# A mixture-of-experts block on one core: one-hot gate rows all on VectorE, gates in four tensors, gathers dealt out by a weighted count

## The chip, the cores and the metric

The kernel runs on one core of one Trainium2 chip. The metric is the device time of one execution in microseconds; lower is better. The core has five engines with a queue each: TensorE (PE, with its weight loads as PEld), VectorE (DVE), ScalarE (ACT), GpSimd (POOL) and SyncE (SP, which here only issues DMAs). An engine takes its instructions in order; engines meet through semaphores.

## The reference, cut to what matters

Two transformer blocks run on 512 tokens of width 1024. The first ends in a product-key expert layer, which is where the change lies:

```python
g = jax.nn.softmax(best_s, axis=-1)                 # 8 heads x 16 chosen experts per token
u = expert_u[idx]                                   # idx = i * 128 + j, out of 16384 experts
act = jax.nn.gelu(jnp.einsum('cd,chkd->chk', xb, u), approximate=False)
w = (g * act).astype(xb.dtype)
return jnp.einsum('chk,chkd->cd', w, expert_v[idx])
```

The kernel treats the tokens in two ways. For the first 128 tokens it gathers the chosen rows of `u` and `v`. For the other 384 (`TD`) it computes the layer densely over all 16384 experts: expert block `b` (0 to 127) holds 128 experts, and a gate that is zero for an expert that was not chosen multiplies the activation.

## The kernel before

**Gate build (about 456 to 644 us).** It makes the dense gates, a matrix of 128 i by 128 j for each of the 384 tokens. Tokens go in 48 groups of 8 (`GS`). `gate_hot(g)` builds three tiles: `oj` and `oi`, one-hot rows of the two indices in fp16 (line 996, VectorE, 128x1024 each), and `og`, `oi` times the gate value (line 1003, 128x1024 out, fp32). Line 1003 runs on GpSimd in every third group (`OGP = 3`) and on VectorE in the others. `oj` and `og` have two buffers (`OGB`), `oi` one. `gate_sum(g)` multiplies them on TensorE, two fp16 matmuls a token (lines 1019 and 1020), into a PSUM bank of four tokens, and ScalarE copies each bank into the staging tile `st` (line 1021): it reads the bank in its own order (token, then i) and writes each element 64 elements (256 bytes) from the one before. `st` holds 64 tokens (`ST`) and has two buffers; when it is full, SP stores its 4 MB in one DMA into the HBM tensor `gates` (line 1023). There are six such stores.

Between the groups TensorE also computes 22 of the `u_side(b)` blocks: 24 matmuls each (lines 199 to 201), whose weights SP loads in pieces of 256 KB (line 93), ScalarE rounds to a high part `wh` (line 111) and GpSimd, in this stretch, subtracts to a low part `wl` (line 112). `Stream` keeps four loads (`WR`) and five split pieces (`WH`) ahead.

**Expert loop (about 644 to 1606 us).** Iteration `b` computes `u_side(b + 34)` (24 matmuls, as long as `b + 34 < 128`, so for b up to 93) and `v_side(b)` (18 matmuls, `vac`). `gate_load(b)` brings 192 KB of gates, 128 rows by six pieces of 256 bytes; `weigh(b)` multiplies them with the activations (line 1052) and splits the product (lines 1054, 1055). Here VectorE makes the low parts of line 112.

In the same loop run the gathered tokens: 256 `units`, 128 rows of `u` and 128 of `v`, each 512 KB by an indirect DMA from GpSimd's queue (line 1077). At most seven row tiles exist (`ROWS`), and a row is worked off five gathers later (`LAG`) by one VectorE instruction over 128x1024 (line 1083 for `u`, 1091 for `v`). How many are issued by iteration b is `due`: an equal number per iteration, all of them by b = 119. At b = 120 (`B_END`) the first 128 tokens get their final norm. What remains of the loop, and the second block, stand behind it.

The lines that deal out the gathers and lay out the gates are:

```python
due = min(len(units), -(-(b + 1) * len(units) // B_END))
gd = nc.dram_tensor("gates", (TD // ST, P, P, ST), FT, kind="Internal").ap()
```

Of the kernel before, what the change touches and what calls it, by code (L numbers as in the profile page):

```python
# [9 lines left out]
FT = mybir.dt.float32  # L10
FR = mybir.dt.float32r
F16 = mybir.dt.float16
# [3 lines left out]
AF = mybir.ActivationFunctionType  # L16
# [4 lines left out]
P = 128  # L21
# [11 lines left out]
TD = S - P  # L33
AA = 36
AHEAD = 34
ST = 64
ROWS, LAG = 7, 5
GS = 8
# [12 lines left out]
LA = 4  # L51
ADA_U = 2
ADA_M = 2
OGP = 3
OGB = 2
U_PRE = 4
B_END = 120
# [100 lines left out]
def body(ctx, tc, a):  # L158
    nc = tc.nc
    V, A, G, T = nc.vector, nc.scalar, nc.gpsimd, nc.tensor  # L160

    def pool(st, name, bufs=1, side="left", **kw):
        return st.enter_context(tc.tile_pool(name=name, bufs=bufs, side=side, reuse_waits="tile", **kw))
# [18 lines left out]
    def rstd(ss, n, inv, nm, bias=None, half=None):  # L182

        u = small.tile([P, n], FT, name=f"rs_u{nm}", tag=f"rs_u{n}")
        last["sqrt"] = A.activation(u, ss, AF.Sqrt, scale=inv, bias=eps if bias is None else bias).ins
        t = small.tile([P, n], FT, name=f"rs_t{nm}", tag=f"rs_t{n}")
        V.tensor_scalar(t, ss, -0.5 * inv, -0.5 * EPS if half is None else half, op0=OP.mult, op1=OP.add)
        r = small.tile([P, n], FT, name=f"rs_r{nm}", tag=f"rs_r{n}")
        V.reciprocal(r, u)
        if n == 1:  # L190
            V.scalar_tensor_tensor(u, r, r, t, op0=OP.mult, op1=OP.mult)
        else:
            V.tensor_mul(u, r, r)
            V.tensor_mul(u, u, t)
        V.scalar_tensor_tensor(r, u, 1.5, r, op0=OP.add, op1=OP.mult)
        return r
# [161 lines left out]
    def rope(pl, ps, raw, rot, cos, sin, nm, rows=slice(0, P), tag="ps", eng=G):  # L358

        pr = ps.tile([P, S], FT, name=f"{nm}pr", tag=tag)  # L360
        T.matmul(pr, con[:, rot - C_RM:rot - C_RM + P], raw, start=True, stop=True)
        t = pl.tile([P, S], FT, name=f"{nm}rt", tag="rt", bufs=2)
        u = pl.tile([P, S], FT, name=f"{nm}ru", tag="ru", bufs=RB)
        eng.tensor_tensor(u[rows], raw[rows], cos[rows], op=OP.mult)
        V.tensor_mul(t[rows], pr[rows], sin[rows])
        V.tensor_add(t[rows], t[rows], u[rows])
        return t

    def rope_swap(pl, raw, cos, sin, nm, eng=G):

        t = pl.tile([P, S], FT, name=f"{nm}rt", tag="rt", bufs=2)
        u = pl.tile([P, S], FT, name=f"{nm}ru", tag="ru", bufs=RB)
        for p0 in range(0, P, 32):
            p1 = p0 + 32 if p0 % 64 == 0 else p0 - 32
            nc.scalar.dma_start(t[p0:p0 + 32], raw[p1:p1 + 32])
        eng.tensor_tensor(u, raw, cos, op=OP.mult)
        V.tensor_mul(t, t, sin)
        V.tensor_add(t, t, u)
        return t
# [86 lines left out]
    i = A.activation(crow, crow, AF.Silu)  # L466
# [34 lines left out]
    with ExitStack() as s1:  # L501
# [10 lines left out]
        for n in range(2):  # L512
            pt = ps.tile([P, 512], FT, name=f"cs{n}", tag="ps")
# [3 lines left out]
        for b0 in (0, 2):  # L517
# [7 lines left out]
            t = rstd(ss, 2, 1.0 / D, f"n1{b0}")  # L525
            r1 += [t[:, 0:1], t[:, 1:2]]
        for b in range(NB):
# [3 lines left out]
            else:  # L531
                i = V.tensor_scalar(xn, x[:, b], r1[b], None, op0=OP.mult)
            if b == 0:
                order.enter_context(tc.issue_after(i.ins))
            for k0 in range(0, KD, 4):
                pt = ps.tile([P, 4, P], FT, name=f"xpt{b}_{k0}", tag="ps")
# [5 lines left out]
        for k in range(KD):  # L542
# [8 lines left out]
            t = p0.tile([P, S], FT, name=f"h1{k}", tag="ht", bufs=2)  # L551
            V.tensor_scalar(t, xnT[:, k], mod[:, k + 8:k + 9], mod[:, k:k + 1], op0=OP.mult, op1=OP.add)
            i = A.activation(hT[:, k], t, AF.Copy)
# [38 lines left out]
        for i in (2, 3):  # L592
# [3 lines left out]
            if i == 2:  # L596
# [13 lines left out]
                for f in (2, 0, 1):  # L610
                    pt = ps.tile([P, S], FT, name=f"lpt{f}", tag="ps")
                    for b in range(NB):
                        T.transpose(pt[:, b * P:(b + 1) * P], lat[:, b, f * P:(f + 1) * P], ident)
                    g = vec[:, V_QN + f:V_QN + f + 1]
# [8 lines left out]
        t = rope_swap(pb, raw_ka, tabs[:, 0], tabs[:, 1], "ka")  # L623
        q_split(t, ks[:, 0], ks[:, 1])
        raws = {0: raw_copy(acc[6], "rawq0")}
        for i in range(4):
            if i < 3:
                raws[i + 1] = raw_copy(acc[7] if i == 0 else qa[i + 1], f"rawq{i + 1}")
            t = rope_swap(pb, raws[i], tabs[:, 0], tabs[:, 1], f"q{i}")
            q_split(t, qs[:, 0, i], qs[:, 1, i])  # L630
            if i == 0:
                t = rope(pb, ps, raw_kr, C_RM, tabm[:, 1], tabm[:, 2], "kr", rows=slice(64, P))
# [5 lines left out]
        for h in range(8):  # L638
            if h % 2 == 0:
                w = ws.get(("qup", h // 2))  # L640
            pt = ps.tile([P, S], FT, name=f"qu{h}", tag="ps")
# [5 lines left out]
        for h in range(8):  # L647
            if h % 4 == 0:
                w = ws.get(("kup", h // 4))
            pt = ps.tile([P, S], FT, name=f"kup{h}", tag="ps")  # L650
# [4 lines left out]
        for b in range(NB):  # L655
            pt = ps.tile([P, 512], FT, name=f"vup{b}", tag="ps")
# [303 lines left out]
    for q in (1, 0, 2):  # L960
        pt = ps.tile([P, 512], FT, name=f"ixT{q}", tag="ps")
# [15 lines left out]
    gp32 = gp.rearrange("p t c -> p (t c)").bitcast(FT)  # L977


    gd = nc.dram_tensor("gates", (TD // ST, P, P, ST), FT, kind="Internal").ap()  # L980
    ps = ps.then(pA=2, pG=4, rest=2)
    s1 = ExitStack()
    pg = pool(s1, "pgb", OGB)
# [7 lines left out]
    def gate_hot(g):  # L991

        tt = slice(g * GS, (g + 1) * GS)

        def hot(out, q):
            V.tensor_tensor(out, iT[:, q, tt].rearrange("p (s t) -> p s t", t=4)[:, :, None].to_broadcast([P, GS // 4, P, 4]),
                            ioth[:, None].to_broadcast([P, GS // 4, P, 4]), op=OP.is_equal)
        oj = pg.tile([P, GS // 4, P, 4], F16, name=f"oj{g}", tag="oj")
        hot(oj, 1)
        oi = pg.tile([P, GS // 4, P, 4], F16, name=f"oi{g}", tag="oi", bufs=1)  # L1000
        hot(oi, 0)
        og = pg.tile([P, GS, P], FT, name=f"og{g}", tag="og")
        (G if g % OGP == 0 else V).tensor_tensor(og.rearrange("p (s t) i -> p s t i", t=4),  # L1003
                        oi.rearrange("p s i t -> p s t i"),
                        gp32[:, tt].rearrange("p (s t) -> p s t", t=4)[:, :, :, None].to_broadcast([P, GS // 4, 4, P]),
                        op=OP.mult)
        return g, oj, og

    stage = {}

    def gate_sum(g, oj, og):
        n, t0 = divmod(g * GS, ST)
        if t0 == 0:
            stage[n] = pg.tile([P, P, ST], FT, name=f"st{n}", tag="st", bufs=2)
        for h in range(GS // 4):
            pt = ps.tile([P, 4, P], FT, name=f"pG{g}_{h}", tag="pG")
            for t in range(4):
                o = og[:, 4 * h + t].bitcast(F16).rearrange("p (i w) -> p i w", w=2)
                T.matmul(pt[:, t], oj[:, h, :, t], o[:, :, 1], start=True, stop=False)  # L1019
                T.matmul(pt[:, t], oj[:, h, :, t], o[:, :, 0], start=False, stop=True)  # L1020
            A.activation(stage[n][:, :, t0 + 4 * h:t0 + 4 * h + 4].rearrange("p i t -> p t i"), pt, AF.Copy)  # L1021
        if t0 + GS == ST:
            nc.sync.dma_start(gd[n], stage.pop(n))

    hot = []
    NG = TD // GS
# [6 lines left out]
    while hot:  # L1033
        gate_sum(*hot.pop(0))
# [3 lines left out]
    pg = pool(s1, "pg", 2)  # L1038
# [5 lines left out]
    gates = {}  # L1044

    def gate_load(b):
        gates[b] = pg.tile([P, TD], FT, name=f"gt{b}", tag="gt", bufs=4)
        nc.sync.dma_start(gates[b].rearrange("p (n t) -> p n t", t=ST), gd[:, :, b].rearrange("n j t -> j n t"))

    def weigh(b):  # L1050
        w = pg.tile([P, TD], FT, name=f"w{b}", tag="w", bufs=1)
        V.tensor_mul(w, acts[:, b % AA], gates.pop(b))  # L1052
        wh, wl = (pg.tile([P, TD], FR, name=f"ww{c}{b}", tag=f"ww{c}", bufs=KL + 1) for c in "hl")
        A.activation(wh, w, AF.Copy)  # L1054
        last["w"] = V.tensor_tensor(wl, w, wh.bitcast(FT), op=OP.subtract).ins  # L1055
        return wh, wl
# [9 lines left out]
    units = []  # L1066
# [41 lines left out]
    t = ps.tags  # L1108
# [3 lines left out]
        gate_load(b)  # L1112
    wts = weigh(0)
    done = 0
    for b in range(P - KL):
        if b + 3 < P:
            gate_load(b + 3)
        if b + AHEAD < P:
            u_side(b + AHEAD)
        v_side((b, *wts, [ws.get(("v", b, n)) for n in range(2)]))  # L1120
        wts = weigh(b + 1)
        due = min(len(units), -(-(b + 1) * len(units) // B_END))
        with tc.issue_after(last["w"]):
            while done < due:
                gather(*units[done])
                done += 1
                if len(rows) > LAG:
                    settle(*rows.pop(0))
            while rows and done == len(units):
                settle(*rows.pop(0))  # L1130
        if b == B_END:

            gf = hn
            mod_row(ps, "pA", gf, 40, "gf")
            y0 = pr.tile([P, D], FT, name="y0", tag="row")
            nc.sync.dma_start(y0, xd[0:P, :])
            fg = pr.tile([P, D], FT, name="fg", tag="row")
            nc.sync.dma_start(fg, a["final_norm"].to_broadcast([P, D]))
            xn0 = pr.tile([P, D], FT, name="xn0", tag="row")
            with tc.issue_after(last["w"]):  # L1140
                V.tensor_mul(acc, acc, gf)
                V.tensor_add(acc, acc, y0)
                r0 = final_norm(0, acc, xn0, fg, y0)
# [34 lines left out]
    for b in range(1, NB):  # L1178
        for n in range(2):
            cl = slice(n * 512, (n + 1) * 512)  # L1180
            t = pf.tile([P, 512], FT, name=f"pt{b}_{n}", tag="pt", bufs=3)
# [30 lines left out]
    if True:  # L1212
# [105 lines left out]
        t = ps.tags  # L1318
# [97 lines left out]
    with ExitStack() as s2:  # L1416
# [13 lines left out]
        for m in range(1, NF):  # L1430
            keys = ("gate", "up")
            pt = {}
# [139 lines left out]
```

## Time and profile before

| | |
|---|---|
| median of 3 runs | 2165.68 us (2163.51 to 2166.59) |
| the profiled execution | 2166.23 us; its span 2164.4 us, so 1.8 us lie around the span |
| busy over the span | PE 2051.1 us (95%), VectorE 1516.6 (70%), ScalarE 925.5 (43%), GpSimd 657.5 (30%) |
| chain of work that ended last | PE 67%, VectorE 17%, DMA 6%, ScalarE 3%, GpSimd 2% |
| gate build, 456 to 644 us | PE 162.99 of 188.00 us at a granted clock of 0.93 |
| loop with both sides, 760 to 1400 us | PE 640.00 of 640.00 us at 1.00 |
| loop with the v side alone, 1437 to 1570 us | PE 119.56 of 133.00 us, DMA share 0.99 |

Times are of one profiled execution. A duration of an instruction can contain a wait for something that the engine shares with another; the start of the next instruction can come shortly before the end of the one before. A DMA share is the mean busy share of the core's 16 DMA engines. [...]

### The profile page before, as it was taken

Reading aid. Unit: us, or ns where it says so; the run is one execution under the profiler, and the core shown is the slowest. Engines: PE = TensorE matmul, PEld = TensorE weight load, DVE = VectorE, ACT = ScalarE, POOL = GpSimd, SP = SyncE. Lnnn points to the kernel's source line nnn. Section 1 sums busy time; section 2 is a strip of 40 time slices with the busy share of each in tenths; the row PEclk is TensorE's granted clock in tenths of the full one; section 3 lists DMA queues with packets and bytes.
Section 4 is the critical chain, followed back from the end, with each engine's and each line's share of the span. In section 5 each row is a group of like instructions: output and inputs, shape, how many; then the busy total and the mean of one; then the engine's idle time right before and its main releaser. Section 6 shows DMA issues by size and latency. Waiting matters only on the chain.

```text
span 2164.4 us, 31580 instructions
## 1 busy us (share of the span) xinstructions
PE 2051.1 (95%) x10907; PEld 1751.0 (81%) x10907; DVE 1516.6 (70%) x3186; ACT 925.5 (43%) x1748; POOL 657.5 (30%) x561
## 2 busy tenths in 40 slices
PE   7999998978888999999999999999889999999999
PEld 5756787878887899999999999986668678888887
DVE  7779879987766776777776777779887855333332
ACT  4477343367663433333333333343353643333321
POOL 2245236675543332323232323234422410000000
PEclk9999999999999999999999999999989999999999
DMA  7515522325559988888889898889953111223332
GB/s 272 179 50 166 175 72 75 104 79 224 209 200 322 329 288 292 283 289 283 282 283 290 284 291 284 289 280 339 353 164 89 49 64 61 96 97 98 98 117 73
DMA packets 264835, 425.91 MB, mean 197 GB/s; under 512 B 119009, under 2 KB 122977, under 8 KB 263906
## 3 DMA queue, kind: packets, MB, share of 16 engines
q1 hardware_dynamic: 222274, 284.15, 40.4%
q0 software_dynamic: 36864, 134.23, 18.1%
q10 hardware_dynamic: 5536, 5.51, 0.9%
q8 instruction: 86, 1.41, 0.3%
q14 instruction: 75, 0.61, 0.1%
HBM read 391.83 MB, written 29.36 MB: 195 GB/s over the span
## 4 chain that ended last, share of the span: by engine, by line
PE 67%; DVE 17%; DMA 6%; issue 3%; ACT 3%; POOL 2%; SPq 0%; ACTq 0%; POOLq 0%; DVEq 0%
PE pA L199 6%; PE pA L200 6%; PE pA L201 6%; PE vac L200 6%; PE vac L201 6%; PE vac L199 6%; DMA wr<-in_v_dram 2%; PE pd L201 2%; PE pd L199 2%; PE pd L200 2%; PE upp L199 2%; PE upp L200 2%; PE upp L201 2%; PE gatep L200 2%; PE gatep L199 2%
## 5 line engine op out<-in xcount | busy, mean ns | idle before, releaser
L111 ACT ACTIVATE wh<-wr 128x512 fp32r<-128x512 f32 x716 | 449.0, 630 | 872.7 <-PE vac L201 234.6
L112 DVE TENSOR_TENSOR wl<-wr,wh 128x512 fp32r<-128x512 f32 x616 | 425.2, 694 | 434.9 <-ACT wh L111 431.6
L199 PE MATMUL pA<-hA,wh 128*128 128x384 f32 x928 | 317.9, 343 | 8.4 <-ACT wh L111 4.3
L201 PE MATMUL pA<-hA,wl 128*128 128x384 f32 x928 | 315.0, 339 | 0.1
L200 PE MATMUL pA<-hA,wh 128*128 128x384 f32 x928 | 314.9, 339 | 0.0
L199 PE MATMUL vac<-wh,wwh 128*128 128x512 f32 x759 | 299.3, 394 | 15.8 <-ACT wwh L1054 13.8
L200 PE MATMUL vac<-wl,wwh 128*128 128x512 f32 x759 | 299.6, 395 | 1.1 <-DVE wl L112 1.1
L201 PE MATMUL vac<-wh,wwl 128*128 128x512 f32 x759 | 296.9, 394 | 0.0
L1077 POOL DMA_INDIRECT ur<-in_u_dram,idx x128 | 151.0, 1180 | 335.2 <-DVE acc L1091 275.0
L1077 POOL DMA_INDIRECT vr<-in_v_dram,idx x128 | 147.7, 1154 | 297.9 <-DVE ur L1083 266.5
L199 PEld LDWEIGHTS pA<-hA,wh 128*128 128x128 f32 x928 | 177.4, 191 | 13.9 <-ACT acts L989 5.4
L199 PEld LDWEIGHTS vac<-wh,wwh 128*128 128x128 f32 x759 | 143.7, 189 | 48.9 <-ACT wwh L1054 18.8
L200 PEld LDWEIGHTS pA<-hA,wh 128*128 128x128 f32 x928 | 177.4, 191 | 3.5
L201 PEld LDWEIGHTS pA<-hA,wl 128*128 128x128 f32 x928 | 177.0, 191 | 0.5 <-DVE wl L112 0.4
L112 POOL TENSOR_TENSOR wl<-wr,wh 128x512 fp32r<-128x512 f32 x100 | 141.1, 1424 | 98.2 <-ACT wh L111 97.9
L201 PEld LDWEIGHTS vac<-wh,wwl 128*128 128x128 f32 x759 | 143.8, 189 | 31.5 <-DVE wwl L1055 1.1
L200 PEld LDWEIGHTS vac<-wl,wwh 128*128 128x128 f32 x759 | 143.6, 189 | 30.1 <-DVE wl L112 2.5
L1091 DVE SCALAR_TENSOR_TENSOR acc<-vr,act,acc 128x1024 f32<-128x1024 f32 x127 | 162.5, 1279 | 0.0
L1083 DVE SCALAR_TENSOR_TENSOR ur<-ur,hn 128x1024 f32<-128x1024 f32 x128 | 155.8, 1219 | 0.0
L1021 ACT ACTIVATE st<-pG 128x512 f32<-128x512 f32 x96 | 94.2, 1125 | 13.0 <-PE pG L1020 12.9
L1054 ACT ACTIVATE wwh<-w 128x384 fp32r<-128x384 f32 x128 | 65.3, 511 | 38.9 <-DVE w L1052 34.6
L1019 PE MATMUL pG<-og,oj 128*128 128x128 f16 x384 | 53.6, 231 | 25.0 <-DVE og L1003 17.6
(678 smaller groups left out, 4065.3 us busy)
## 6 DMA issues: line engine op xcount, KB each, us to landing
wr<-in_uT_dram SPq DMA_DIRECT2D x256, 256.0 KB
wr<-in_v_dram SPq DMA_DIRECT2D x256, 256.0 KB
wa<-in_w_adaT_dram SPq DMA_DIRECT2D x48, 512.0 KB
gates<-st SPq DMA_DIRECT2D x6, 4096.0 KB
gt<-gates SPq DMA_DIRECT2D x128, 192.0 KB
wr<-in_w_gate_dram SPq DMA_DIRECT2D x44, 256.0 KB
wr<-in_w_up_dram SPq DMA_DIRECT2D x44, 256.0 KB
wr<-in_w_down_dram SPq DMA_DIRECT2D x44, 256.0 KB
```

Source lines behind the costliest of these rows:

```text
L111: self.nc.scalar.activation(hi, raw, AF.Copy)
L112: (lo_eng or self.nc.vector).tensor_tensor(lo, raw, hi.bitcast(FT), op=OP.subtract)
L199: T.matmul(out, lh, rh, start=start, stop=False)
L200: T.matmul(out, lh, rl, start=False, stop=False)
L201: return T.matmul(out, ll, rh, start=False, stop=stop).ins
L1019: T.matmul(pt[:, t], oj[:, h, :, t], o[:, :, 1], start=True, stop=False)
L1021: A.activation(stage[n][:, :, t0 + 4 * h:t0 + 4 * h + 4].rearrange("p i t -> p t i"), pt, AF.Copy)
L1054: A.activation(wh, w, AF.Copy)
L1077: G.indirect_dma_start(out=r, out_offset=None, in_=a[kind], in_offset=bass.IndirectOffsetOnAxis(ap=idx[:, j:j + 1], axis=0))
L1083: V.scalar_tensor_tensor(r, r, 1.0, hn, op0=OP.mult, op1=OP.mult, accum_out=act[:, j:j + 1])
L1091: V.scalar_tensor_tensor(acc, r, act[:, j:j + 1], acc, op0=OP.mult, op1=OP.add)
```

## The change

Five edits:

1. Line 1003 (`og`) runs on VectorE in all 48 groups; GpSimd did 16 of them. `OGP` goes.
2. `oi` has two buffers (the pool's count) where it had one.
3. The copy of line 1021 goes through the bank in the order (i, token): it writes runs of four adjacent elements into `st`, and reads PSUM in steps of 128 elements.
4. `gates` becomes four HBM tensors of 32 expert blocks each; a store becomes four DMAs of 1 MB; `gate_load(b)` reads from tensor `b // 32` and so depends on that tensor's stores alone. The step from one row to the next in HBM goes from 32 KB to 8 KB.
5. `due` follows `pace`, which counts an iteration with a u side twice and one without once: 256 units over a count of 215, up to b = 120. That is 2.38 gathers per iteration up to b = 93 and 1.19 after it, in place of 2.13 throughout.

```diff
--- before.py
+++ after.py
@@ -51,7 +51,6 @@
 LA = 4
 ADA_U = 2
 ADA_M = 2
-OGP = 3
 OGB = 2
 U_PRE = 4
 B_END = 120
@@ -977,7 +976,7 @@
     gp32 = gp.rearrange("p t c -> p (t c)").bitcast(FT)
 
 
-    gd = nc.dram_tensor("gates", (TD // ST, P, P, ST), FT, kind="Internal").ap()
+    gd = [nc.dram_tensor(f"gates{q}", (TD // ST, P, P // 4, ST), FT, kind="Internal").ap() for q in range(4)]
     ps = ps.then(pA=2, pG=4, rest=2)
     s1 = ExitStack()
     pg = pool(s1, "pgb", OGB)
@@ -997,10 +996,10 @@
                             ioth[:, None].to_broadcast([P, GS // 4, P, 4]), op=OP.is_equal)
         oj = pg.tile([P, GS // 4, P, 4], F16, name=f"oj{g}", tag="oj")
         hot(oj, 1)
-        oi = pg.tile([P, GS // 4, P, 4], F16, name=f"oi{g}", tag="oi", bufs=1)
+        oi = pg.tile([P, GS // 4, P, 4], F16, name=f"oi{g}", tag="oi")
         hot(oi, 0)
         og = pg.tile([P, GS, P], FT, name=f"og{g}", tag="og")
-        (G if g % OGP == 0 else V).tensor_tensor(og.rearrange("p (s t) i -> p s t i", t=4),
+        V.tensor_tensor(og.rearrange("p (s t) i -> p s t i", t=4),
                         oi.rearrange("p s i t -> p s t i"),
                         gp32[:, tt].rearrange("p (s t) -> p s t", t=4)[:, :, :, None].to_broadcast([P, GS // 4, 4, P]),
                         op=OP.mult)
@@ -1018,9 +1017,11 @@
                 o = og[:, 4 * h + t].bitcast(F16).rearrange("p (i w) -> p i w", w=2)
                 T.matmul(pt[:, t], oj[:, h, :, t], o[:, :, 1], start=True, stop=False)
                 T.matmul(pt[:, t], oj[:, h, :, t], o[:, :, 0], start=False, stop=True)
-            A.activation(stage[n][:, :, t0 + 4 * h:t0 + 4 * h + 4].rearrange("p i t -> p t i"), pt, AF.Copy)
+            A.activation(stage[n][:, :, t0 + 4 * h:t0 + 4 * h + 4], pt.rearrange("p t i -> p i t"), AF.Copy)
         if t0 + GS == ST:
-            nc.sync.dma_start(gd[n], stage.pop(n))
+            st = stage.pop(n)
+            for q in range(4):
+                nc.sync.dma_start(gd[q][n], st[:, q * (P // 4):(q + 1) * (P // 4)])
 
     hot = []
     NG = TD // GS
@@ -1045,7 +1046,7 @@
 
     def gate_load(b):
         gates[b] = pg.tile([P, TD], FT, name=f"gt{b}", tag="gt", bufs=4)
-        nc.sync.dma_start(gates[b].rearrange("p (n t) -> p n t", t=ST), gd[:, :, b].rearrange("n j t -> j n t"))
+        nc.sync.dma_start(gates[b].rearrange("p (n t) -> p n t", t=ST), gd[b // 32][:, :, b % 32].rearrange("n j t -> j n t"))
 
     def weigh(b):
         w = pg.tile([P, TD], FT, name=f"w{b}", tag="w", bufs=1)
@@ -1112,6 +1113,8 @@
         gate_load(b)
     wts = weigh(0)
     done = 0
+
+    pace = np.cumsum([2 if b + AHEAD < P else 1 for b in range(P)]).tolist()
     for b in range(P - KL):
         if b + 3 < P:
             gate_load(b + 3)
@@ -1119,7 +1122,7 @@
             u_side(b + AHEAD)
         v_side((b, *wts, [ws.get(("v", b, n)) for n in range(2)]))
         wts = weigh(b + 1)
-        due = min(len(units), -(-(b + 1) * len(units) // B_END))
+        due = min(len(units), -(-pace[b] * len(units) // pace[B_END]))
         with tc.issue_after(last["w"]):
             while done < due:
                 gather(*units[done])
```

## Rows read from the trace of the kernel before

**Rows 1.** Four stretches: busy time of each engine (instructions), granted clock, DMA

```profile
core 0: us, PE busy (x) PEld busy (x) DVE busy (x) ACT busy (x) POOL busy (x), PEclk, DMA share, GB/s
456.00:644.00 188.00, 162.99 (x1354) 156.79 (x1353) 145.85 (x135) 131.41 (x174) 102.98 (x61) 0.93 0.49 184
644.00:722.00 78.00, 69.63 (x330) 61.52 (x329) 52.69 (x93) 27.59 (x51) 28.64 (x25) 0.96 1.00 338
760.00:1400.00 640.00, 640.00 (x3238) 582.65 (x3237) 459.10 (x716) 248.38 (x468) 190.07 (x166) 1.00 0.88 286
1437.00:1570.00 133.00, 119.56 (x502) 93.92 (x501) 116.52 (x172) 46.89 (x86) 57.71 (x47) 0.97 0.99 335
```

**Rows 2.** Waits from 456 to 644 us: total, times, longest

```profile
POOL og L1003 <- DVE oi L996: 32.0, 11, 4.9
DVE oi L996 <- POOL og L1003: 30.2, 15, 3.1
...
PE pG L1019 <- DVE og L1003: 17.6, 9, 2.9
...
DVE oj L996 <- PE pG L1020: 5.9, 5, 2.5
```

**Rows 3.** Instructions in order of time, gate build: start, duration, engine and line

```profile
500.48 1.30 POOL L112 TENSOR_TENSOR wl<-wr,wh 128x512 fp32r<-128x512 f32 x1 [1.56 <-ACT wh L111]
500.53 1.79 DVE L996 TENSOR_TENSOR oj<-iT,ioth 128x1024 f16<-128x1024 f16 x1
...
509.58 1.22 DVE L1003 TENSOR_TENSOR og<-oi,gp 128x1024 f32<-128x1024 f16 x1
...
510.72 0.68 DVE L996 TENSOR_TENSOR oj<-iT,ioth 128x1024 f16<-128x1024 f16 x1
...
511.32 0.68 DVE L996 TENSOR_TENSOR oi<-iT,ioth 128x1024 f16<-128x1024 f16 x1
```

**Rows 4.** The tile og: minimum, median and maximum duration in ns

```profile
L1003 POOL TENSOR_TENSOR og<-oi,gp x16: 1903/2202/2376, 459.1 to 628.7; 128x1024 f32<-128x1024 f16 x16
```

**Rows 5.** Groups of GpSimd in the gate build

```profile
L112 POOL TENSOR_TENSOR wl<-wr,wh 128x512 fp32r<-128x512 f32 x44 | 68.3, 1561 | 41.0 <-ACT wh L111 40.9
```

**Rows 6.** Groups of ScalarE in the whole span: two copies out of PSUM

```profile
L1021 ACT ACTIVATE st<-pG 128x512 f32<-128x512 f32 x96 | 94.2, 1125 | 13.0 <-PE pG L1020 12.9
...
L859 ACT ACTIVATE qy<-qp 128x512 f32<-128x512 f32 x16 | 9.3, 578 | 0.0
```

**Rows 7.** The chain that ended last, from 640 to 665 us: start, duration, what

```profile
643.78 12.08 DMA gates<-st
```

**Rows 8.** DMA queues and issues, 760 to 1400 us

```profile
q1 hardware_dynamic: 104770, 95.98, 47.9%
q0 software_dynamic: 23760, 86.52, 40.2%
...
gt<-gates SPq DMA_DIRECT2D x77, 192.0 KB
```

**Rows 9.** DMA queues and issues, 1437 to 1570 us

```profile
q0 software_dynamic: 6897, 25.11, 52.4%
q1 hardware_dynamic: 25338, 19.30, 46.5%
...
wr<-in_v_dram SPq DMA_DIRECT2D x54, 256.0 KB
```

**Rows 10.** TensorE in order of time: two matmuls, eighteen places apart

```profile
1445.00 0.39 PE L199 MATMUL vac<-wh,wwh 128*128 128x512 f32 x1
...
1449.08 0.39 PE L199 MATMUL vac<-wh,wwh 128*128 128x512 f32 x1
```

**Rows 11.** Groups of VectorE, 1437 to 1570 us

```profile
L1091 DVE SCALAR_TENSOR_TENSOR acc<-vr,act,acc 128x1024 f32<-128x1024 f32 x32 | 40.9, 1279 | 0.0
L112 DVE TENSOR_TENSOR wl<-wr,wh 128x512 fp32r<-128x512 f32 x54 | 36.5, 688 | 16.0 <-ACT wh L111 14.6 <-issue 1.3
...
L1055 DVE TENSOR_TENSOR wwl<-w,wwh 128x384 fp32r<-128x384 f32 x23 | 12.7, 554 | 3.0 <-ACT wwh L1054 2.4 <-issue 0.6
```

## Prediction

> **What bounds the kernel now.** I read the stretches first [rows 1], then the waits and single instructions of the gate build [rows 2 to 6], then the DMA of the loop [rows 7 to 9] and its last part [rows 10, 11]. The reader should see four stretches with four different limits.
>
> In the gate build no engine looks full: TensorE 163 of 188 us, VectorE 146, ScalarE 131, GpSimd 103 [rows 1]. But VectorE and GpSimd don't work side by side. A one-hot instruction takes 0.68 us with GpSimd idle and 1.79 us when GpSimd's `wl` started 0.05 us before it and ran for 1.30 us [rows 3]: it waited for that to end. So their work adds up. Prices alone, from start to start: one-hot 0.60 (510.72 to 511.32), `og` on VectorE 1.14 (509.58 to 510.72) [rows 3], `og` on GpSimd 1.90 [rows 4], `wl` on GpSimd 1.30 [rows 3]. The 44 `wl` of this stretch have a mean of 1.56 [rows 5], which contains such waits, so I don't use it. Counts: 48 groups give 96 one-hots, 32 `og` on VectorE and 16 on GpSimd; five `wl` on VectorE by my count of the stretch, 0.6 each. Sum: 57.6 + 36.5 + 30.4 + 57.2 + 3.0 = 184.7 of 188 us. One of the two is at work nearly throughout, and the two also wait for each other through the single `oi`: 32.0 and 30.2 us [rows 2]. TensorE's waits for `og` follow from that.
>
> From 644 to 722 us the DMA is full (share 1.00) and TensorE has 69.6 of 78 us [rows 1]. The last 4 MB store takes 12.08 us [rows 7], and everything that the loop needs stands behind it. From 760 to 1400 us TensorE is busy without a gap at full clock, DMA share 0.88 [rows 1]. From 1437 us the iterations are half as long for TensorE and still carry 2.13 gathers: the DMA share is 0.99 and TensorE has 119.6 of 133 us [rows 1].
>
> **The change, part by part.**
>
> *`og` all on VectorE, two `oi`.* Sixteen instructions of 1.90 us leave the common resource and sixteen of 1.14 come: 16 x 0.76 = 12.2 us. The new sum is 172.5 us; with the same 3.3 us in which neither works the stretch is 175.8 in place of 188. TensorE's 163 us contain its own slow spells (clock 0.93), so it stays below that. What is late next is TensorE: VectorE waits for it through the two `oj` and `og` buffers, 5.9 us now [rows 2], and will more often, since it no longer waits for GpSimd. Ends: 25 us gained (the stretch falls to TensorE's 163) and 0 (TensorE's turns take all that comes free). A loss I exclude here: no instruction is added, and the `wl` that GpSimd now runs between VectorE's instructions are split ahead of need. I take 12, the exchange of prices. The second `oi` has no gain of its own beside that: in order on one engine, the reader of `oi` is always done before the next is written.
>
> *The staging copy.* 96 copies at 1.125 us now; a copy of the same size out of PSUM, contiguous on both sides, takes 0.578 [rows 6]. So stepping by 256 bytes on the SBUF side costs about 0.55 us. The new copy writes runs of four and steps in PSUM instead, which no row shows. Its price lies between 0.578 and 0.578 + 2 x 0.547 = 1.67 us (the step in PSUM dearer, by the same amount again). ScalarE has 131.4 - 94.2 = 37 us of other work in the stretch, so it would be busy 93 to 198 us. It stays hidden below (175.8 - 37) / 96 = 1.44 us. I take 0.6 to 1.13, nearest to the two copies that the trace has, and nothing for the sum; what hides it is the common resource of VectorE and GpSimd.
>
> [...]
>
> *Four tensors, four stores.* The bytes stay; 18 more DMA issues on SP, which mostly waits in this stretch. The first gate loads need 1 MB of the last 4, so 3.0 us in place of 12.08 if they ran ahead; but they are issued to the same queue behind the other 3 MB, and the DMA is full there [rows 1, 7]. Ends: 9 us and nothing; I take 2. The loads read the same pieces of 256 bytes at another row step. Their price can be bounded: one iteration of q1 costs 0.479 x 640 / 77 = 3.98 us of all engines with four loads of 256 KB and one gate load [rows 8], and 0.465 x 133 / 27 = 2.29 with two and one [rows 9]; the difference gives 0.85 a load and leaves about 0.6 for a gate load, up to 0.9 if a load costs what its bytes cost in the other stretch. I keep it.
>
> *Gathers by time.* A gather costs 0.402 x 640 / 166 = 1.55 us of all DMA engines in the long stretch [rows 1, 8] and 0.524 x 133 / 47 = 1.48 in the last [rows 1, 9].
> Long stretch: an iteration needs 3.98 + 2.13 x 1.55 = 7.28 us of DMA within 8.31 us of TensorE (640 / 77); after, 3.98 + 2.38 x 1.55 = 7.67. VectorE goes from 459 / 640 = 0.72 to 0.72 + 0.25 x 1.28 / 8.31 = 0.76 [rows 1, 11]. TensorE's work hides both: cost 0. Without that cover each 0.1 us an iteration would cost 9 us over 94.
> Last part: 27 iterations (54 loads) and 47 gathers, 27 x 2.29 + 47 x 1.48 = 131.5 of the 133 us: the DMA sets its length. By the old count 209 gathers are out after b = 97 or so; the new count has 229 there (192 of 215 shares of 256) and leaves 27. DMA after: 61.8 + 40.0 = 102 us. TensorE: 27 x 4.08 = 110 us [rows 10]. VectorE per iteration: 2 x 0.69 + 2 x 0.55 + 1.19 x 1.28 = 4.0 of 4.08 us, durations that overlap a little [rows 11]. So TensorE bounds it, with the two others just below; I allow 7 us for their unevenness: 117, a gain of 16. Ends: 23 (110 us) and 5 (128 us, the three in each other's way). At the end five rows wait as before, but they are now worked off at b = 120, in the same turn as the final norm, not one earlier: +2 us, between 0 and 5.
> Start: about eight iterations up to 722 us bring two more gathers while the DMA is full: +3 us, between 0 and 3.
>
> *Sum*, against the profiled execution: 2166.2 - 12 (build) - 16 + 2 (last part) - 2 + 3 (start) = 2141 us. The median lies 0.55 us below that execution, less than I can resolve: 2141.
>
> **The rivals.**
> *Only the gathers help.* The build's pace is set by the turns between VectorE and TensorE, not by the sum of prices: 5.9 us of waits for TensorE speak for it, 62 us between VectorE and GpSimd against [rows 2]. 2166 - 13 = 2153.
> *Only the build helps.* The last part stays uneven, because DMA (102) and VectorE (27 x 4.0 = 108) are close under TensorE's 110: gain 3 there. 2166 - 12 - 3 + 1 = 2152.
> *The copy becomes the bound.* At 1.67 us ScalarE has 198 us of work in the build: +10 there, -13 from the gathers: about 2163. For it: the step in PSUM is new and long. Against: no row shows such a price. [...]
> *Slower: the loop's DMA fills up.* Place: iterations 10 to 93, now 7.28 of 8.31 us. With 7.67 there are 0.64 us left; if the gate loads cost twice as much at the new row step (+0.9 us), an iteration takes 8.57: 94 x 0.26 = +24 us, the last part needs 102 + 24 = 126 of DMA and gains 7 less 2, and the time is 2166 - 12 + 24 - 5 + 1 = 2174. It decides against the change from about 8.5 us an iteration. For it: this is the one transfer of the loop whose step in HBM changes. Against: the pieces stay, and TensorE had no gap at 0.88.
> *That the change doesn't do what it says* can be for the four tensors alone, in the sum at 2 us.
>
> **How the numbers follow.** Two runs of this kernel can be told apart from about 0.2%, 4.3 us. Forecast (both parts help) 0.60; only gathers 0.13; only the build 0.09; copy 0.06, which lies between "same" and a little faster; slower 0.12, with smaller faults of the start in it. Faster by over 0.2%: 0.60 + 0.13 + 0.09 = 0.82; within: 0.06; slower: 0.12. The range goes from 2127 (build -20, last part -19) to 2158, past both half cases; the copy and the slower case stay outside.
>
> **What would show it.** Right: no `og` on GpSimd, `oi` never waiting, the stretch up to the last store near 176 us, and 27 v iterations in about 117 us at a DMA share well under 0.99 with fewer than 30 gathers. Wrong: a long stretch with gaps on TensorE or a share near 1.0 (the DMA); copies above 1.44 us; VectorE's wait for `pG` grown to some 20 us (turns); the start longer than 78 us by more than 3.

## The result and the profile after

The changed kernel takes 2125.96 us (median of 4 runs, 2121.77 to 2134.0) against 2166.14 (4 runs): ratio 0.9825, 95% interval 0.9805 to 0.9845. That is 40 us faster where 25 were forecast, and 1 us under the low end of the range. The profiled execution has 2124.07 us, its span 2122.3.

The stretches of the changed kernel, with the columns of [rows 1] (line numbers of the changed kernel are one lower up to the gate build, one higher in the loop):

```profile
core 0: us, PE busy (x) PEld busy (x) DVE busy (x) ACT busy (x) POOL busy (x), PEclk, DMA share, GB/s
...
461.80:629.30 167.50, 154.20 (x1345) 146.90 (x1344) 163.59 (x150) 90.10 (x172) 80.85 (x45) 0.98 0.56 205
629.30:716.00 86.70, 78.12 (x370) 69.77 (x369) 59.47 (x102) 30.22 (x56) 33.61 (x28) 0.94 1.00 338
716.00:1420.00 704.00, 703.75 (x3559) 640.37 (x3559) 531.46 (x819) 274.74 (x517) 240.21 (x201) 1.00 0.92 303
1420.00:1567.00 147.00, 146.28 (x656) 120.31 (x655) 126.94 (x204) 67.43 (x126) 38.24 (x32) 1.00 0.84 271
```

Cut at the same events, before and after: the start of the first one-hot row, the end of the last staging copy, the starts of the activations that end the 9th, the 29th and the last u side behind the build, and the end of the last v side. Each length below is the difference of two such times.

| us | before | after | forecast of the change |
|---|---|---|---|
| up to the first one-hot row (no edit) | 456.5 | 461.8 | 0 |
| gate build | 187.2 | 167.5 | -12 |
| build to 9th u side | 86.4 | 87.1 | +1 |
| 9th to 29th u side | 163.2 | 164.9 | 0 |
| 29th to last u side | 539.9 | 539.2 | 0 |
| last u side to last v side | 172.2 | 146.7 | -14 |
| rest (no edit) | 558.9 | 555.2 | 0 |

The build gave 20 us and the last part 25; the first and the last line are not touched by any edit and differ by +5.3 and -3.7.

In the build, VectorE is now busy nearly without a break: 163.6 of 167.5 us. Its three groups, and then GpSimd's, which is left with `wl` alone; columns are the count, busy us and mean ns, idle time before:

```profile
L1002 DVE TENSOR_TENSOR og<-oi,gp 128x1024 f32<-128x1024 f16 x48 | 73.6, 1534 | 0.0
L995 DVE TENSOR_TENSOR oi<-iT,ioth 128x1024 f16<-128x1024 f16 x48 | 55.8, 1197 | 0.1
L995 DVE TENSOR_TENSOR oj<-iT,ioth 128x1024 f16<-128x1024 f16 x48 | 40.0, 833 | 0.5 <-PE pG L1019 0.4
```
GpSimd:

```profile
L111 POOL TENSOR_TENSOR wl<-wr,wh 128x512 fp32r<-128x512 f32 x44 | 79.9, 1819 | 76.0 <-ACT wh L110 76.0
```

No `og` stands on GpSimd any more. The mean of `oi` (1197 ns) and `og` (1534) against 0.68 and 1.22 us alone [rows 3] is where `wl` gets in between, as in these three instructions in order of time: `og` starts 0.59 us into a `wl` and takes 2.32 us.

```profile
502.39 0.68 DVE L995 TENSOR_TENSOR oj<-iT,ioth 128x1024 f16<-128x1024 f16 x1
502.40 1.83 POOL L111 TENSOR_TENSOR wl<-wr,wh 128x512 fp32r<-128x512 f32 x1 [2.82 <-ACT wh L110]
...
502.99 2.32 DVE L1002 TENSOR_TENSOR og<-oi,gp 128x1024 f32<-128x1024 f16 x1
```

The waits that answer to [rows 2] are gone or smaller: VectorE waits for no `og`, and for TensorE 0.4 us where it had been 5.9. GpSimd just waits for work.

```profile
POOL wl L111 <- ACT wh L110: 76.0, 41, 7.2
...
PE pG L1018 <- DVE og L1002: 13.2, 18, 1.8
...
DVE oj L995 <- PE pG L1019: 0.4, 1, 0.4
```

The staging copy, group of ScalarE in the build, to be held against [rows 6]: 599 ns in place of 1125, next to the 578 of the contiguous copy.

```profile
L1020 ACT ACTIVATE st<-pG 128x512 f32<-128x512 f32 x96 | 51.3, 599 | 13.9 <-PE pG L1019 13.9
```

In the last part TensorE is busy throughout, 124.00 of 124.00 us at a granted clock of 1.00 (a share of full speed), where it had 119.56 of 133.00 at 0.97 [rows 1]; below it the DMA queues there, then the long stretch and its queues:

```profile
1424.00:1548.00 124.00, 124.00 (x555) 102.50 (x554) 109.05 (x168) 54.24 (x103) 31.42 (x26) 1.00 0.90 289
```

```profile
q1 hardware_dynamic: 28667, 22.05, 57.2%
q0 software_dynamic: 3744, 13.63, 32.5%
...
wr<-in_v_dram SPq DMA_DIRECT2D x60, 256.0 KB, 5.2
```

```profile
760.00:1400.00 640.00, 640.00 (x3238) 582.74 (x3237) 482.47 (x745) 249.25 (x470) 219.57 (x183) 1.00 0.92 301
```

```profile
q1 hardware_dynamic: 105338, 96.07, 46.9%
q0 software_dynamic: 26437, 96.27, 44.4%
...
gt<-gates SPq DMA_DIRECT2D x77, 192.0 KB, 5.9
```

The last part carries 3744 packets of the gathers' queue (q0) in 124 us where it had 6897 in 133 [rows 9]; the long stretch 26437 where it had 23760 [rows 8], and TensorE's busy time there is 640.00 of 640.00 us as before.

### The profile page after: what moved, and what is told of

It is laid out like the page before. It is cut to its first block, busy times and chain, and to the rows that moved or that the text cites. A ratio compares the mean times of both kernels' runs of the same rounds, so it can differ in the third digit from the quotient of the medians.

```text
span 2122.3 us, 31628 instructions
## 1 busy us (share of the span) xinstructions
PE 2033.1 (96%) x10907; PEld 1738.9 (82%) x10907; DVE 1540.5 (73%) x3202; ACT 884.8 (42%) x1748; POOL 645.1 (30%) x545
## 3 DMA queue, kind: packets, MB, share of 16 engines
q0 software_dynamic: 36864, 134.23, 18.5%
## 4 chain that ended last, share of the span: by engine, by line
PE 72%; DVE 19%; DMA 3%; issue 2%; ACT 2%; POOL 1%; SPq 0%; ACTq 0%; DVEq 0%; POOLq 0%
PE vac L199 7%; PE vac L200 7%; PE vac L198 7%; PE pA L198 6%; PE pA L199 6%; PE pA L200 6%; DVE og L1002 3%; DVE oi L995 2%; PE pd L199 2%; PE pd L198 2%; PE pd L200 2%; PE upp L200 2%; PE upp L199 2%; PE upp L198 2%; PE gatep L199 2%
## 5 line engine op out<-in xcount | busy, mean ns | idle before, releaser
L1078 POOL DMA_INDIRECT ur<-in_u_dram,idx x128 | 157.8, 1233 | 298.0 <-DVE acc L1092 236.0
L1078 POOL DMA_INDIRECT vr<-in_v_dram,idx x128 | 149.0, 1164 | 294.6 <-DVE ur L1084 251.6
L111 POOL TENSOR_TENSOR wl<-wr,wh 128x512 fp32r<-128x512 f32 x100 | 153.4, 1543 | 132.6 <-ACT wh L110 132.4
L1053 DVE TENSOR_TENSOR w<-acts,gt 128x384 f32<-128x384 f32 x128 | 71.0, 555 | 5.6 <-DMA gt<-gates 5.5
L1056 DVE TENSOR_TENSOR wwl<-w,wwh 128x384 fp32r<-128x384 f32 x128 | 70.8, 553 | 4.4 <-ACT wwh L1055 4.1
```

Source lines behind the costliest of these rows:

```text
L111: (lo_eng or self.nc.vector).tensor_tensor(lo, raw, hi.bitcast(FT), op=OP.subtract)
L1078: G.indirect_dma_start(out=r, out_offset=None, in_=a[kind], in_offset=bass.IndirectOffsetOnAxis(ap=idx[:, j:j + 1], axis=0))
```

## The experiments

Two theories were set against each other. By theory A the build is as long as VectorE's and GpSimd's work together, since one blocks the other, and the last part was as long as its DMA work. By the rivals the build was paced by engines taking turns (single `oi`, copies ahead of the weights on ScalarE), and other edits had a share in the last part. All times are medians against the runs of the kernel before on the same chip (2164.1 to 2166.3 us); stage lengths are cut as in the table above, each from the one profiled execution of its run.

| run | time | ratio (95%) | build | last part |
|---|---|---|---|---|
| e1: only the new count | 2144.07 | 0.9899 (0.9883 to 0.9916) | 187.3 | 146.7 |
| e2: all but the new count | 2144.33 | 0.9899 (0.9883 to 0.9916) | 167.2 | 170.4 |
| e3: old staging copy | 2126.94 | 0.983 (0.9807 to 0.9853) | 168.2 | 146.6 |
| e4: every third `og` on GpSimd | 2137.1 | 0.988 (0.9861 to 0.99) | 182.9 | 146.6 |
| e5: one `oi` | 2127.2 | 0.9821 (0.9796 to 0.9845) | 167.9 | 147.0 |
| e6: one gate tensor | 2121.26 | 0.9793 (0.977 to 0.9817) | 167.2 | 147.4 |
| e7: `wl` of the build on VectorE | 2103.59 | 0.9726 (0.9701 to 0.975) | 149.0 | 146.7 |
| e8: no gather behind the last u side | 2123.18 | 0.9813 (0.979 to 0.9836) | 167.6 | 146.8 |
| e9: e7, no gather in six iterations | 2100.27 | 0.9697 (0.9677 to 0.9717) | 148.8 | 147.3 |
| e10: e7, one gate tensor | 2105.49 | 0.9737 (0.971 to 0.9765) | 149.0 | 146.7 |
| e11: before, `wl` on VectorE | 2134.74 | 0.9862 (0.9841 to 0.9883) | 159.7 | 168.6 |
| e12: the changed kernel again | 2125.84 | 0.9823 (0.98 to 0.9846) | 167.6 | 147.9 |

**e1 and e2: the two halves apart.** e1 is the kernel before with edit 5, e2 the changed kernel without it:

```diff
-        due = min(len(units), -(-(b + 1) * len(units) // B_END))
+        due = min(len(units), -(-pace[b] * len(units) // pace[B_END]))
```

> The kernel before with edit 5 alone (gathers dealt out by the weighted count). Theory A (the last part of the loop was bound by the DMA, and the new count alone frees it): the last part from the last u side to the last v side goes from 172 to about 147 us, the gate build stays at 187 us, time 25 us under before (2138 to 2144). Rival (the four gate tensors, with their shorter row step, take part in the freed last part): at least a third of the 25 us is missing, time above 2148.

> The changed kernel with the old count of gathers, so edits 1 to 4 alone. Theory A: gate build 167 us, the last part back at about 172 us, time 12 to 18 us under before (2148 to 2154). Rival (an earlier first gate load and the shorter row step carry over into the loop): the last part comes below 165 us, time under 2146.

e1 gains 21.5 us and has the short last part with the old gates, so the four tensors have no share in it; the time lies just past the 2138 to 2144 us expected. e2 gains 21.3 us, more than the 12 to 18 expected, and has the short build and the long last part. Its time is under the rival's 2146 us, but the last part of 170.4 us, which the rival had below 165, speaks against it. The halves add up to 42.8 us, against 40.2 and 40.5 for the whole (first runs and e12).

**e3: the copy as it was.**

```diff
-            A.activation(stage[n][:, :, t0 + 4 * h:t0 + 4 * h + 4], pt.rearrange("p t i -> p i t"), AF.Copy)
+            A.activation(stage[n][:, :, t0 + 4 * h:t0 + 4 * h + 4].rearrange("p i t -> p t i"), pt, AF.Copy)
```

> The changed kernel with the staging copy of before (edit 3 undone): ScalarE writes in steps of 256 bytes again, 1.1 us a copy in place of 0.6. Theory A (the build is VectorE plus GpSimd, ScalarE is hidden): build 167 to 170 us, time within 3 us of the changed kernel. Rival (the shorter copy gives back the 8 us by which the build beat the forecast, since the weights' high parts no longer wait behind copies): build about 176 us, time 6 to 10 us above the changed kernel.

The build takes 0.7 us more, the time is the changed kernel's. The copy is hidden, with the code of the changed kernel (599 ns a copy there) or of the kernel before (1125 ns there); the rival falls.

**e4: `og` back on GpSimd in every third group, two `oi`.**

```diff
-        V.tensor_tensor(og.rearrange("p (s t) i -> p s t i", t=4),
+        (G if g % 3 == 0 else V).tensor_tensor(og.rearrange("p (s t) i -> p s t i", t=4),
```

> The changed kernel with every third og back on GpSimd (edit 1 undone), two oi buffers kept. Theory A (the work of VectorE and GpSimd adds up): 16 x 0.76 = 12 us more, build 178 to 182 us, time 12 us above the changed kernel. Rival (turns: VectorE stood still for the single oi, which the second buffer cures): build 167 to 171 us, time within 4 us of the changed kernel.

15.4 of the build's 19.7 us go again (182.9 us where 178 to 182 were expected), so the place of `og` is most of the gain and the turns around the single `oi` are not. What is above the 12.2 us of exchanged prices shows in the waits of this run (engine waiting, for whom, total, times, longest): turns that the changed kernel doesn't have.

```profile
DVE oj L995 <- PE pG L1019: 11.1, 4, 3.3
POOL og L1002 <- PE pG L1019: 8.9, 3, 3.7
...
DVE oi L995 <- POOL og L1002: 6.7, 3, 3.0
```

**e5: one `oi` again**, all on VectorE (`bufs=1` back on `oi`).

> The changed kernel with a single oi buffer (edit 2 undone), og still all on VectorE. Theory A: in order on one engine nobody waits for oi, so nothing changes: build 166 to 169 us, time within 4 us of the changed kernel. Rival (the second oi is a part of the gain by itself): build 171 us or more.

No change: the build takes 167.9 us where it had 167.5, so on one engine, in order, the second buffer has nothing to do. Beside an `og` on GpSimd it may be worth something: the kernel before and e4 differ by 4.3 us in the build, through edits 2 to 5 together, and no run has the second `oi` alone there.

**e6: one gate tensor, one store** (edit 4 undone).

```diff
-            st = stage.pop(n)
-            for q in range(4):
-                nc.sync.dma_start(gd[q][n], st[:, q * (P // 4):(q + 1) * (P // 4)])
+            nc.sync.dma_start(gd[n], stage.pop(n))
```

> The changed kernel with one HBM tensor for the gates and one 4 MB store for each stage (edit 4 undone). The forecast had 2 us for four tensors. By the runs so far the first v side starts 18.7 to 20 us after the last staging copy with four tensors and 17.6 to 17.8 with one. Theory A: no gain in the split, time within 4 us of the changed kernel, first v side 17 to 20 us after the last copy. Rival (the split frees the start, something else hides it): first v side over 25 us after the last copy, time 5 us or more above.

The first v side starts 18.6 us after the last copy, in the band of the others. The time is 4.7 us under the changed kernel's, outside the 4 us that were expected; e10 asks again. Why the split brings nothing can be seen in the changed kernel. SP issues the four stores at 629.30 and the first gate loads at 637.83, 8.5 us later; before, they went out when the store of [rows 7] had landed, after 12.1 us:

```profile
629.30 4.55 SPq L1024 DMA_DIRECT2D gates<-st  x4
...
637.83 9.88 SPq L1049 DMA_DIRECT2D gt<-gates  x5
```

but VectorE has the gates only at 646.77, 17.5 us after the stores were issued (before: 659.99 less 643.78, 16.2 us). After, then before:

```profile
646.77 0.56 DVE L1053 TENSOR_TENSOR w<-acts,gt 128x384 f32<-128x384 f32 x1 [0.66 <-DMA gt<-gates]
```

```profile
659.99 0.56 DVE L1052 TENSOR_TENSOR w<-acts,gt 128x384 f32<-128x384 f32 x1 [0.79 <-DMA gt<-gates]
```

The loads are issued earlier and land no earlier. The trace has the times from issue to landing, here of the last of the four stores (issued at 632.68) and of the first gate load (637.83):

```profile
gates<-st SPq DMA_DIRECT2D x1, 1024.0 KB, 9.6
...
gt<-gates SPq DMA_DIRECT2D x1, 192.0 KB, 8.9
```

The first store lands at 634.9, the last at 642.3, then the three weight loads that SP issued between stores and gate loads (644.7, 645.3, 646.0), then the first gate load, at 646.7. The second store's landing isn't in the trace; the gate load landed behind all the others that stood ahead of it in SP's queue, stores that it doesn't need included.

**e7: the low parts of the build on VectorE too.**

```diff
     for b in range(len(u_at), AHEAD):
-        add_u(b, lo=G)
+        add_u(b, lo=G if b < n_early else None)
```

> The changed kernel with the 44 low parts wl of the build on VectorE as well, so that GpSimd has no work of its own in it. Theory A (the two engines exclude each other, so what counts is the sum): 44 x about 1.1 us of GpSimd leave the sum and 44 x 0.6 come, 167 - 22 = 145 us of VectorE, and TensorE becomes the bound: build 148 to 156 us, time 11 to 19 us under the changed kernel. Rival (VectorE's own list is the bound, busy 163.6 of 167.5 us now, and GpSimd's work is free beside it): build 167 + 26 = 193 us, time 20 to 26 us above the changed kernel.

This separates the theories by over 30 us, and A holds: VectorE gets 26 us more of its own to do and the build gets 18.5 us shorter. The time falls by 22 us, more than the 11 to 19 expected; 5.8 us of it lie ahead of the build, where nothing was edited. One-hots and `og` come down to their lone durations, and TensorE is the bound, at a granted clock of 1.00. The stretch, then VectorE's groups from 456 to 620 us:

```profile
456.00:605.00 149.00, 149.00 (x1343) 144.38 (x1342) 142.41 (x193) 87.82 (x171) 2.19 (x1) 1.00 0.63 230
```

```profile
L1002 DVE TENSOR_TENSOR og<-oi,gp 128x1024 f32<-128x1024 f16 x48 | 58.8, 1225 | 0.0
...
L995 DVE TENSOR_TENSOR oj<-iT,ioth 128x1024 f16<-128x1024 f16 x48 | 33.1, 690 | 0.0
L995 DVE TENSOR_TENSOR oi<-iT,ioth 128x1024 f16<-128x1024 f16 x48 | 32.2, 692 | 0.0
```

**e8: all gathers under the u sides** (`pace` counts 1 and 0 in place of 2 and 1).

> The changed kernel with all gathers dealt out over the iterations that have a u side: 2.72 in each up to b = 93, none after. DMA work per long iteration by the forecast's prices: 3.98 + 2.72 x 1.55 = 8.20 of 8.31 us. Theory A (the DMA work of an iteration against TensorE's 8.31 us decides): the long stretch stays within 1% of TensorE's pace after the start, the start loses 5 to 10 us because the backlog has little to drain into, the last part stays at about 146 us or gains 2, time 3 to 10 us above the changed kernel. Rival (the average says little, since the DMA's unevenness costs well before 100%): gaps on TensorE all along, long stretch 20 us or more longer.

It costs nothing, where 3 to 10 us were expected (2123.18 us against 2125.96): from the 9th to the 29th u side 2 us more than the changed kernel, and no gap in the long stretch at a DMA share of 0.96:

```profile
760.00:1400.00 640.00, 640.00 (x3237) 582.68 (x3236) 518.23 (x781) 249.94 (x471) 265.13 (x207) 1.00 0.96 324
```

So both theories were too careful: in this stretch the DMA's unevenness doesn't reach TensorE even at that share.

**e9: e7 with no gather due before iteration 6** (`pace` counts 0 there).

> The kernel of e7 (all of the build's elementwise work on VectorE) with no gather due in the first six iterations of the loop; 2.52 per long iteration after them, 1.26 at the end. Theory A (from the last store on, the start is bound by the DMA, which carries the 4 MB store, the loads and the first gathers at once): some 14 rows of 1.5 us leave it, the first eight u sides after the build (83 us in the changed kernel, 66.5 at TensorE's pace) take 70 to 78 us, time 5 to 12 us under e7. Rival (the start waits for the store and the first gates, whatever else is on the DMA): 80 us or more, time within 4 us of e7.

The eight u sides take 76.6 us in place of e7's 80.8, as expected by A; the next twenty take 1.8 us more, and the time is 3.3 us less, short of the 5 and within what the rival had; the two intervals overlap. The first gathers are a part of what the start costs: TensorE still lacks 6.7 of 77 us with the DMA at 0.92. The stretch in e9, then in e7:

```profile
609.00:686.00 77.00, 70.28 (x341) 62.53 (x342) 45.73 (x79) 28.85 (x55) 16.38 (x16) 0.98 0.92 291
```

```profile
609.00:690.00 81.00, 73.38 (x353) 64.45 (x354) 58.96 (x101) 29.50 (x56) 33.17 (x28) 0.98 1.04 349
```

**e10: e7 with one gate tensor** (e7 and e6 together).

> The kernel of e7 with one HBM tensor for the gates (edit 4 undone). Theory A: the split is worth nothing here either, time within 4 us of e7. Rival (one tensor is better, as the 4 to 5 us between e6 and the changed kernel's first runs hint): 4 us or more under e7, with the first v side earlier after the last staging copy.

1.9 us above e7 where e6 had been 4.7 below the changed kernel: no sign that holds. The split is worth nothing that can be measured.

**e11: the kernel before with e7's line alone.**

> The kernel before with nothing changed but the 44 low parts wl of the build on VectorE. Theory A (VectorE and GpSimd add up): 44 x (1.1 - 0.6) = 22 us out of 187, a build of 163 to 170 us, time 17 to 24 us under before: about as much as the build edits of this change bring. Rival (what held the build before was the turn-taking over the single oi, not the sum): VectorE still stands still for og on GpSimd, build 178 us or more.

The build takes 159.7 us, less than the 167.5 of the changed kernel, with `og` still on GpSimd and a single `oi`; the time falls by 31.6 us. Both are more than was expected (163 to 170 us, and 17 to 24 us under before). VectorE's wait for `og` shrinks from 30.2 us [rows 2] to 9.1, since GpSimd no longer has `wl` to do ahead of it:

```profile
DVE oi L996 <- POOL og L1003: 9.1, 5, 1.8
```

```profile
457.20:616.90 159.70, 151.67 (x1348) 146.59 (x1347) 143.05 (x177) 129.48 (x171) 35.73 (x17) 0.99 0.58 215
```

So the turns were a consequence of the sum: GpSimd was late because of its own list and the blocking.

**e12: the yardstick.**

> The changed kernel once more, unaltered, as the yardstick of this call: 2122 to 2130 us, build 167 us, last part 147 us.

2125.84 us, build 167.6, last part 147.9, as expected.

## Why the prediction was right, and where its sizes were off

**The build.** The mechanism was right (e4, e7). The term was mis-sized, 12 us for 19.7, in the step that added the prices to 184.7 of 188 us and left 3.3 us in which neither worked. The price of `wl` in it, 1.30 us, is its duration on GpSimd; what VectorE loses to one is less. In the changed kernel VectorE works nearly without a break for the 162.8 us from the first one-hot row to the end of its last `og`. Its own list up to there, at the prediction's prices, is 57.6 + 54.7 + 1.8 = 114.1 us (three of the five `wl`), so its instructions lasted 162.2 - 114.1 = 48.1 us longer than alone: 1.09 us for each of the 44 `wl`. The same stretch before and after, with the columns of [rows 1] (VectorE's busy time is the third of the engines'):

```profile
456.53:637.77 181.24, 156.23 (x1307) 150.35 (x1306) 143.96 (x132) 125.84 (x166) 102.63 (x61) 0.93 0.50 187
```

```profile
461.81:624.63 162.82, 149.52 (x1310) 142.54 (x1309) 162.19 (x148) 87.47 (x167) 80.84 (x45) 0.98 0.57 208
```

Before, the own list is 57.6 + 36.5 + 1.8 = 95.9 of 144.0 busy us, so the instructions were longer by the same 48.1 us. What the move took away is VectorE's idle time, 37.3 us before and 0.6 after, and what it cost is 18.2 us of own work. The idle time before stands at the end of these lines:

```profile
L996 DVE TENSOR_TENSOR oi<-iT,ioth 128x1024 f16<-128x1024 f16 x48 | 53.9, 1123 | 30.7 <-POOL og L1003 30.2
L996 DVE TENSOR_TENSOR oj<-iT,ioth 128x1024 f16<-128x1024 f16 x48 | 51.4, 1071 | 5.9 <-PE pG L1020 5.9
```

The 30.7 us of waiting for GpSimd's `og`, less the 18.2, are the exchange that was forecast at 12.2. The other 5.9 us are the wait for TensorE, of which the prediction said that it would come more often; it fell to 0.4. With `og` partly on GpSimd it stays, two `oi` or not (11.1 us in e4). The last 1.3 us lie behind the last `og`, where the stretch goes on for 4.7 us in place of 6.0. Nor was TensorE's time of 163 us a floor, as the far end of 25 us had it: e7 has 149.0, at a granted clock of 1.00 in place of 0.93.

**The staging copy.** Nothing in the sum, as forecast, and e3 shows it. The price is 0.60, at the low end of 0.58 to 1.67. The high end, with the step in PSUM dearer than the one in SBUF, was my estimate, and the trace doesn't show it: stepping by 512 bytes through PSUM cost ScalarE next to nothing here, 599 ns a copy against 578 contiguous. The rival in which the copy became the bound falls.

**Four tensors.** -2 was forecast; e6 and e10 find nothing. The end that I had named, loads behind the other stores, is what the landing times under e6 show. The slower rival needed a gate load of twice the price: in the long stretch q1 takes 0.469 x 640 / 77 = 3.90 us an iteration where it took 3.98, so the new row step shows no cost.

**Gathers by time.** The long stretch hides them, as forecast: DMA share 0.92 (7.67 / 8.31), no gap. In the last part the mis-sized step is "I allow 7 us for their unevenness", with the 2 us for the later final norm: TensorE has no gap at all with the DMA share at 0.90, so the whole 23 us of the far end came, and 2.5 more in the iterations behind it, where TensorE had probably been held up by the rows that are worked off at the end (argued from the order on VectorE, not tried). TensorE's own busy time fell too, with the granted clock at 1.00 in place of 0.97: here is the last part before, to be held against 146.28 of 147.00 us after.

```profile
1433.00:1605.50 172.50, 155.87 (x654) 122.50 (x652) 150.49 (x235) 68.27 (x125) 63.99 (x53) 0.97 0.89 298
```

e8 says the same for the long stretch. The start's 3 us can't be told from scatter: from the build to the 29th u side the time grew by 2.4 us here and 3.1 in e1, but in e12, the same kernel as here, it was 0.3 us shorter than before.

Build and last part both came out larger than forecast, 7.7 and 11.5 us, and so the time lies under the range.

**What stays open.** The stretches that no edit touches differ from kernel to kernel, 454.3 to 461.8 us ahead of the build and 555.2 to 560.8 behind the loop, with no cause found. Ahead of the build the difference goes with the kernel: the changed kernel has 461.8 us and, in e12, 460.7, e2 has 461.0, all others 454.3 to 457.5. So differences of 3 to 5 us between two of these kernels, as e6's, say little.

Best of all runs is e9 (0.9697), with e7 not to be told from it (0.9726).

## What to carry to other kernels

When two engines block each other, add their work and look at the sum; a small instruction on the "free" engine may cost the busy one more than doing it itself (here 1.09 us lost for 0.6 us of work), so moving more work to the engine that looks fullest can shorten the stretch (by 18.5 us in e7). Deal out side work by the time of an iteration and not by its number: a stretch whose DMA is full and another with spare share next to it is time left lying (shares of 0.99 and 0.88 here; the new count alone gained 21.5 us in e1). And where a stretch shows no gap at a share of 0.88 with several buffers ahead, don't charge a surcharge for unevenness on a share of 0.92 (e8 had no gap at 0.96 either).

## What the runs showed of the hardware that was not expected

- A `wl` of 1.30 us on GpSimd held VectorE up for 1.09 us on average (48.1 us over 44), and its own duration rose to a mean of 1.82 us; the one that started 0.01 us behind a one-hot row of 0.68 us took 1.83.
- ScalarE read a PSUM bank in steps of 512 bytes at nearly the price of a contiguous copy (599 and 578 ns), while stepping by 256 bytes on the SBUF side had cost it 0.55 us over 512 elements a partition (1125 ns against 578).
- 2.72 gathers of 512 KB an iteration beside the loads, a DMA share of 0.96 over 640 us, left TensorE without a gap (640.00 of 640.00 us busy, e8).
